# A gMLP's products over positions, from full-width operands to three products of split ones

## The chip, the core and the metric

The kernel runs on one core of a Trainium2 chip. The metric is the time of one execution on the device in microseconds (us); the median of several timed runs is compared. A profile is one further execution, recorded instruction by instruction. The engines are named as in the profile: PE (TensorE, matrix products), PEld (its weight loads, which run beside the products), DVE (VectorE), ACT (ScalarE), POOL (GpSimd) and SP (which here only issues DMAs). Each of them works through its own queue in order.

## What is computed

Two layers of a decoder trunk over 256 positions and 1024 features. The change lies in the third mixer of each layer, a gMLP:

```python
def chunked_spatial_gating(u_pre, v_pre, ln_g, ln_b, w_s, b_s):
    u = jax.nn.gelu(u_pre, approximate=False)
    v = layer_norm(jax.nn.gelu(v_pre, approximate=False), ln_g, ln_b)
    n = S // GMLP_CHUNK                      # 2 chunks of 128 positions
    vc = v.reshape(B, n, GMLP_CHUNK, GMLP_GROUPS, GMLP_GROUP_DIM)   # 8 groups of 128 features
    w_causal = w_s * tril[None]
    sp = jnp.einsum('gij,bnjgc->bnigc', w_causal, vc) + b_s.T[None, None, :, :, None]
    return u * sp.reshape(B, S, GMLP_WIDTH)
```

So each group has one 128x128 causal matrix over positions, which is applied to both chunks: 16 products of 128x128 by 128x128 per layer, 32 in all. Around them stand the large projections of the layer: the input projection to 12800 columns, the three branch projections, the output projection and a SwiGLU block, all in float32 accuracy.

## The kernel before

All large projections are done in a split form. An operand is parted into a high half of few mantissa bits (an ACT copy into the type fp32r) and the rest (a DVE subtraction); the function `split` (lines 196 and 197) emits these two instructions. A product then is three products of halves: high by high, high by low, low by high. `mm3` emits them (lines 268, 269, 270), for results that have features on the partitions; `toks` does the same for results with positions there (lines 288 to 290). `feat` makes one 256-feature block of a projection: 16 calls of `mm3` with 256 moving columns.

Weights stream in from DRAM as panels (1 MB each, tile `raw`), and each panel is cut into four pieces of 128x512, each split into `wh` and `wl`. The recording order is made by hand: a step of the list `steps` is one `feat` or a few `toks` with what follows on ACT and DVE, and while a step's products are emitted, `spend` counts their nanoseconds and calls `tick` once in 1300 of them. A tick emits one callback from the queue `hooks`, perhaps one part of the attention from `slow`, and zero to two pieces of weights, by how far the pieces are ahead of the products. Each engine then runs what it was given in this order, with semaphores between engines.

The stretch around the change, in each layer:

- `conv(j, which)` for j = 0 to 3 and which = 0, 1, 2: a `feat` each; with which = 2 the result on PSUM is multiplied into `cy` on DVE (line 744) and split into `yah` (ACT) and `yal` (DVE).
- `spatial`, called in `conv(2, 0)`, loads the causal matrices `ws` and the biases `bs` by hooks; two later hooks multiply the matrices by the triangle (line 485).
- `gu(j)` for j = 0 to 3, right after `conv(3, 2)`: first four products over positions for two groups and two chunks (line 764: stationary `gv`, which is v, moving `ws`, both plain float32), then the bias on DVE (line 768, tile `sp`), then a `feat` for u, its Gelu, the product u by `sp`, and the split into `ych` and `ycl`.

The attention of the same layer (`scores`, `turn`, `pv`) runs spread between these steps. Tiles of 128x512 come from two pools of slots, 48 and 24; `room` stops the making of pieces when few slots are left.

Of the kernel before, what the change touches and what calls it, by code (L numbers as in the profile page):

```python
# [12 lines left out]
F32R = mybir.dt.float32r  # L13
# [86 lines left out]
def trunk(ctx: ExitStack, tc: tile.TileContext, a, out):  # L100
    nc = tc.nc
# [16 lines left out]
    def flat(name, dt=F32, at=None):  # L118

        if at is None:  # L120
            y = sum(n.startswith("y") for n in home)
            at = int(not name.startswith(('va', 'qk', 'ws', 'bs')) and live[1] + (cnt["y"] - y if cnt["y"] else 0) < NS[1])
        live[at] += 1
        assert live[at] <= NS[at], (name, live)
        s = sl[at].tile([128, 512], dt, tag=f"slot{at}", name=name)
        home[s.tensor.name] = at
        return s

    def slot(name, dt=F32, at=None):
        return flat(name, dt, at).rearrange("p (b s) -> p b s", b=2)  # L130

    def free(*tiles):
        for s in tiles:
            live[home.pop(s.tensor.name)] -= 1
# [4 lines left out]
    def acc():  # L139
        return pa.tile([128, 512], F32, tag="acc", name="acc")  # L140
# [53 lines left out]
    def split(h, l, src):  # L194

        nc.scalar.activation(h, src, AF.Copy)  # L196
        V.tensor_tensor(l, src, h.bitcast(F32), op=OP.subtract)  # L197
# [20 lines left out]
    hooks = deque()  # L218
# [47 lines left out]
    def mm3(o, hl, rhs_h, rhs_l, first, last):  # L266

        nc.tensor.matmul(o, lhsT=hl[0], rhs=rhs_h, start=first, stop=False)  # L268
        nc.tensor.matmul(o, lhsT=hl[0], rhs=rhs_l, start=False, stop=False)  # L269
        nc.tensor.matmul(o, lhsT=hl[1], rhs=rhs_h, start=False, stop=last)  # L270

    def feat(p, rhs):

        ps = acc()
        for b in range(2):
            for k in range(p.kc):
                mm3(ps[:, b * S:(b + 1) * S], p.at(k, b * 128, 128), *rhs(k), k == 0, k == p.kc - 1)
                if b == 1 and k % 2 == 1:
                    used()
                if b == 0 or k < p.kc - 1:  # L280
                    spend(327)
        spend(327)
        return ps.rearrange("p (b s) -> p b s", b=2)
# [167 lines left out]
    def layer(L, steps):  # L451
        first, final = L == 0, L == DEPTH - 1
        w_in = a["w_in"][L]
        st = {}
# [40 lines left out]
        v_t = {}  # L495
# [50 lines left out]
        c = OFF_V  # L546
# [31 lines left out]
        for g in range(NG):  # L578
            c = OFF_ATT + (3 * g + 2) * GCOL
# [139 lines left out]
        def conv(j, which):  # L719
            def f(P):  # L720
                ps = feat(P[0], xf)
                cw = st["cw"]
                if which == 0:
                    if j == 0:
                        cnt["y"] = 20
                    if j == 2:
                        st["spatial"]()
                    st["c"] = slot("cc")
                    nc.scalar.activation(st["c"], ps, AF.Copy)
                elif which == 1:  # L730
                    z = st["c"]
                    y = st["y"] = slot("cy")
                    V.tensor_tensor(z, z, ps, op=OP.mult)
                    for i in (2, 1, 0):
                        for b in range(2):
                            w, n = cw[:, i, 2 * j + b:2 * j + b + 1], 2 - i
                            if n == 0:
                                V.tensor_scalar(y[:, b, :], z[:, b, :], w, None, op0=OP.mult)
                            else:
                                V.scalar_tensor_tensor(y[:, b, n:], z[:, b, :S - n], w, y[:, b, n:], op0=OP.mult, op1=OP.add)  # L740
                    free(z)
                else:
                    y = st["y"]
                    V.tensor_tensor(y, y, ps, op=OP.mult)
                    ya[j] = (slot(f"yah{j}", F32R, 1), slot(f"yal{j}", F32R, 1))
                    split(ya[j][0], ya[j][1], y)
                    free(y)
            return f
# [4 lines left out]


        yc = {}

        def gu(j):
            def f(P):
                sp = acc()
                for b in range(2):  # L760
                    g = 2 * j + b
                    for n in range(2):
                        vv = v_t[n, g // 4][:, (g % 4) * 128:(g % 4 + 1) * 128]
                        nc.tensor.matmul(sp[:, (2 * b + n) * 128:(2 * b + n + 1) * 128], lhsT=vv, rhs=st["wsT"][g // 4][:, g % 4, :], start=True, stop=True)  # L764
                s = slot("sp")
                for b in range(2):
                    g = 2 * j + b
                    V.tensor_tensor(s[:, b, :].rearrange("p (n i) -> p n i", n=2),
                                    sp[:, b * 256:(b + 1) * 256].rearrange("p (n i) -> p n i", n=2),
                                    st["bs"][g // 4][:, None, (g % 4) * 128:(g % 4 + 1) * 128].to_broadcast([128, 2, 128]), op=OP.add)  # L770
                ps = feat(P[0], xf)
                u = slot("u")
                nc.scalar.activation(u, ps, AF.Gelu)
                V.tensor_tensor(u, u, s, op=OP.mult)
                yc[j] = (slot(f"ych{j}", F32R, 1), slot(f"ycl{j}", F32R, 1))
                split(yc[j][0], yc[j][1], u)
                free(u, s)
                if j == 3:
                    free(*v_t.values(), *st["wsT"], *st["bs"])
            return f  # L780
# [41 lines left out]
        for j in range(4):  # L822
            n = slice(j * 256, (j + 1) * 256)
# [128 lines left out]
    for L in range(DEPTH):  # L952
        n = len(steps)
        starts[n] = layer(L, steps)
# [76 lines left out]
```

## Time and profile before

| | us |
|---|---|
| median of 3 timed runs (1135.79 to 1136.28) | 1135.81 |
| the profiled execution, its own time | 1134.36 |
| its span from first to last instruction | 1132.6 |
| PE busy | 1119.3 (99% of the span) |
| PEld busy | 1056.1 (93%) |
| DVE busy | 776.7 (69%) |
| ACT busy | 618.3 (55%) |
| mean granted clock of PE, as a share of full speed | 0.997 |

A row of the timeline gives the start in us from the start of the span, the duration, the engine, the line in the kernel, the operation, the tiles (out<-in), the shape and how many instructions the row joins. In a shape such as 128\*128 128x256 the first part is the stationary operand and the second the result. Consecutive products overlap in the engine's pipeline, so the pace of PE is read from start to start and not from the durations. In square brackets stands an idle time of the engine before the row and what ended it.

### The profile page before, as it was taken

What the parts mean: (1) busy time and instruction counts of PE and PEld (TensorE: products, weight loads), DVE (VectorE), ACT (ScalarE), POOL (GpSimd) and SP (SyncE); (2) the same over time, 40 slices, a digit from 0 to 9 for tenths busy, and PEclk for the clock granted to TensorE, in tenths of its full rate; (3) what the DMA queues carried; (4) which work ended last, traced back from release to release, by engine and by line L of the source; (5) the groups of instructions that cost most, each with busy time, mean ns of one, the idle gap of its engine ahead of it and who ended that gap; (6) DMA issues with size and microseconds to landing.
All of it is one profiled execution on the core that took longest, in us unless ns stands there. A gap on an engine that the chain in (4) does not pass through costs nothing.

```text
span 1132.6 us, 21868 instructions
## 1 busy us (share of the span) xinstructions
PE 1119.3 (99%) x8822; PEld 1056.1 (93%) x8822; DVE 776.7 (69%) x1401; ACT 618.3 (55%) x1139; POOL 58.2 (5%) x120
## 2 busy tenths in 40 slices
PE   9899999999999999999999999999999999999997
PEld 7799999999999899998888999999999998999985
DVE  6979786677555875556698677667675569655554
ACT  7565665666444374545387356566654445544550
POOL 0013200000002000000000232000000010000000
PEclk9999999999999999999999999999999999999999
DMA  9589555369557475546358575454666655745541
GB/s 323 167 269 295 161 170 192 124 212 309 170 178 272 160 262 187 181 156 242 125 179 297 170 224 167 150 197 150 210 237 206 199 192 190 257 157 179 186 149 38
DMA packets 175781, 223.35 MB, mean 197 GB/s; under 512 B 5824, under 2 KB 146368, under 8 KB 175680
## 3 DMA queue, kind: packets, MB, share of 16 engines
q1 hardware_dynamic: 169904, 209.36, 55.0%
q0 software_dynamic: 4672, 11.54, 3.5%
q8 instruction: 69, 1.13, 0.4%
q10 hardware_dynamic: 1104, 1.05, 0.3%
q14 instruction: 32, 0.26, 0.1%
HBM read 214.59 MB, written 1.05 MB: 190 GB/s over the span
## 4 chain that ended last, share of the span: by engine, by line
PE 98%; DVE 1%; DMA 0%; ACT 0%; issue 0%; ACTq 0%
PE acc L268 22%; PE acc L269 22%; PE acc L270 22%; PE acc L289 9%; PE acc L290 9%; PE acc L288 9%; PE trp L661 1%; PE acc L671 1%; PE trp L633 1%; PE acc L764 1%; PE trp L337 0%; PE trp L641 0%; PE acc L677 0%; DMA xT<-in_xT 0%; PE trp L872 0%
## 5 line engine op out<-in xcount | busy, mean ns | idle before, releaser
L197 DVE TENSOR_TENSOR wl<-raw,wh 128x512 fp32r<-128x512 f32 x776 | 496.7, 686 | 210.4 <-ACT wh L196 188.0
L268 PE MATMUL acc<-xh,wh 128*128 128x256 f32 x1856 | 517.0, 279 | 0.0
L270 PE MATMUL acc<-xh,wl 128*128 128x256 f32 x1856 | 512.5, 276 | 0.0
L269 PE MATMUL acc<-xl,wh 128*128 128x256 f32 x1856 | 512.5, 276 | 0.0
L196 ACT ACTIVATE wh<-raw 128x512 fp32r<-128x512 f32 x776 | 439.4, 623 | 103.3 <-PE acc L269 30.8
L268 PEld LDWEIGHTS acc<-xh,wh 128*128 128x128 f32 x1856 | 348.4, 188 | 1.2
L269 PEld LDWEIGHTS acc<-xl,wh 128*128 128x128 f32 x1856 | 348.5, 188 | 0.1
L270 PEld LDWEIGHTS acc<-xh,wl 128*128 128x128 f32 x1856 | 348.4, 188 | 0.0
L600 POOL DMA_DIRECT2D sw<-qk x96 | 47.3, 500 | 421.2 <-ACT qk L598 421.0
L288 PE MATMUL acc<-wh,hh 128*128 128x512 f32 x176 | 68.7, 390 | 0.0
L290 PE MATMUL acc<-wh,hl 128*128 128x512 f32 x176 | 68.5, 389 | 0.0
L289 PE MATMUL acc<-wl,hh 128*128 128x512 f32 x176 | 68.5, 389 | 0.0
L288 PE MATMUL acc<-wh,xh 128*128 128x512 f32 x128 | 50.9, 398 | 0.8 <-ACT wh L196 0.8
L289 PE MATMUL acc<-wl,xh 128*128 128x512 f32 x128 | 50.2, 392 | 0.2 <-DVE wl L197 0.2
L290 PE MATMUL acc<-wh,xl 128*128 128x512 f32 x128 | 50.3, 393 | 0.0
L289 PE MATMUL acc<-wl,xrh 128*128 128x512 f32 x96 | 38.3, 399 | 2.9 <-DVE wl L197 2.9
L290 PEld LDWEIGHTS acc<-wh,hl 128*128 128x128 f32 x176 | 33.0, 188 | 6.9
L288 PEld LDWEIGHTS acc<-wh,hh 128*128 128x128 f32 x176 | 33.0, 188 | 6.8
L289 PEld LDWEIGHTS acc<-wl,hh 128*128 128x128 f32 x176 | 33.1, 188 | 6.7
L290 PE MATMUL acc<-wh,xrl 128*128 128x512 f32 x96 | 38.3, 399 | 0.0
L288 PE MATMUL acc<-wh,xrh 128*128 128x512 f32 x96 | 38.1, 397 | 0.0
L797 ACT ACTIVATE sg<-acc 128x512 f32<-128x512 f32 x24 | 14.3, 597 | 42.7 <-PE acc L270 42.7
(157 smaller groups left out, 1331.9 us busy)
## 6 DMA issues: line engine op xcount, KB each, us to landing
raw<-in_w_in SPq DMA_DIRECT2D x98, 1024.0 KB, 5.0
raw<-in_w_gate SPq DMA_DIRECT2D x22, 1024.0 KB, 5.0
raw<-in_w_up SPq DMA_DIRECT2D x22, 1024.0 KB, 5.0
raw<-in_w_down SPq DMA_DIRECT2D x22, 1024.0 KB, 4.8
raw<-in_p_a SPq DMA_DIRECT2D x8, 1024.0 KB, 5.4
raw<-in_p_c SPq DMA_DIRECT2D x8, 1024.0 KB, 5.0
raw<-in_w_o SPq DMA_DIRECT2D x8, 1024.0 KB, 6.3
sw<-qk POOLq DMA_DIRECT2D x96, 64.0 KB, 3.3
```

The source lines that it names most:

```text
L196: nc.scalar.activation(h, src, AF.Copy)
L197: V.tensor_tensor(l, src, h.bitcast(F32), op=OP.subtract)
L268: nc.tensor.matmul(o, lhsT=hl[0], rhs=rhs_h, start=first, stop=False)
L269: nc.tensor.matmul(o, lhsT=hl[0], rhs=rhs_l, start=False, stop=False)
L270: nc.tensor.matmul(o, lhsT=hl[1], rhs=rhs_h, start=False, stop=last)
L288: nc.tensor.matmul(ps, lhsT=lhs[0], rhs=h, start=first, stop=False)
L289: nc.tensor.matmul(ps, lhsT=lhs[0], rhs=l, start=False, stop=False)
L290: nc.tensor.matmul(ps, lhsT=lhs[1], rhs=h, start=False, stop=last)
L600: nc.gpsimd.dma_start(sw[o:o + 32], r[i:i + 32])
L633: nc.tensor.matmul(ps[t, r][:, :S], lhsT=q[d, b, own[t]], rhs=k[d, b, :], start=(i == 0), stop=(i == 2))
L661: nc.tensor.transpose(ps[:, i * 128:(i + 1) * 128], p[:, i * 128:(i + 1) * 128], ident)
L797: nc.scalar.activation(s, ps, AF.Sigmoid)
```

## The change

`gu` no longer multiplies float32 tiles. A new function `vw_parts(j)` takes three slots, `vsh` and `vsl` for the halves of v (two chunks by 256 features) and `wsp` for both halves of two causal matrices, and puts two callbacks at the end of `hooks`: `values` splits v (two `split` of 128x256), `matrices` splits the two causal matrices (one `split` of 128x256). It is called for j = 0 at the end of the last `conv` step, and for j + 1 at the start of `gu(j)`. At its start, `gu(j)` takes callbacks from `hooks` until its own halves have been emitted. Each of the four products is an `mm3` with 128 moving columns.

```diff
@@ def conv(j, which): def f(P):
             ps = feat(P[0], xf)
             cw = st["cw"]
+            if which == 2 and j == 3:
+                vw_parts(0)
...
         yc = {}
+        vw = {}
+
+        def vw_parts(j):
+
+            vh, vl, w = (slot(n, F32R) for n in ("vsh", "vsl", "wsp"))
+            vw[j] = [vh, vl, w, False]
+            c = slice(j % 2 * 256, j % 2 * 256 + 256)
+
+            def values():
+                for n in range(2):
+                    split(vh[:, n], vl[:, n], v_t[n, j // 2][:, c])
+
+            def matrices():
+                split(w[:, 0], w[:, 1], st["wsT"][j // 2].rearrange("p g j -> p (g j)")[:, c])
+                vw[j][-1] = True
+
+            hooks.extend((values, matrices))
 
         def gu(j):
             def f(P):
+                while not vw[j][-1]:
+                    hooks.popleft()()
+                vh, vl, w, _ = vw.pop(j)
+                if j < 3:
+                    vw_parts(j + 1)
                 sp = acc()
                 for b in range(2):
-                    g = 2 * j + b
+                    c = slice(128 * b, 128 * b + 128)
                     for n in range(2):
-                        vv = v_t[n, g // 4][:, (g % 4) * 128:(g % 4 + 1) * 128]
-                        nc.tensor.matmul(sp[:, (2 * b + n) * 128:(2 * b + n + 1) * 128], lhsT=vv, rhs=st["wsT"][g // 4][:, g % 4, :], start=True, stop=True)
+                        mm3(sp[:, (2 * b + n) * 128:(2 * b + n + 1) * 128], (vh[:, n, c], vl[:, n, c]), w[:, 0, c], w[:, 1, c], True, True)
+                free(vh, vl, w)
                 s = slot("sp")
```

How this moves the instructions is shown at two engines, both at the border from `conv(3, 2)` to `gu(0)` in layer 0; layer 1 has the same rows with other numbers. In brackets stands which engine's semaphore an instruction waits for. First PE, of before:

```order
L270 MATMUL acc<-xh,wl 128x256
L764 MATMUL acc<-ws_2399,gv_274 128x128
L764 MATMUL acc<-ws_2399,gv_277 128x128
L764 MATMUL acc<-ws_2399,gv_274 128x128
L764 MATMUL acc<-ws_2399,gv_277 128x128
```

The same place on PE in the changed kernel:

```order
L268 MATMUL acc<-wsp,vsh 128x128 [waits Activation_49]
L269 MATMUL acc<-wsp,vsh 128x128 [waits DVE_49]
L270 MATMUL acc<-wsp,vsl 128x128
L268 MATMUL acc<-wsp,vsh 128x128
L269 MATMUL acc<-wsp,vsh 128x128
L270 MATMUL acc<-wsp,vsl 128x128
L268 MATMUL acc<-wsp,vsh 128x128
```

Twelve products stand where four stood, and the first two of them wait for ACT and for DVE, where the four waited for neither. Now DVE, from the multiplication of the last `conv` step's result on, before:

```order
L744 TENSOR_TENSOR cy<-cy,acc 128x512 [waits DVE_49,PE_49]
L197 TENSOR_TENSOR yal_2877<-cy,yah_2876 128x512 [waits Activation_49]
L768 TENSOR_TENSOR sp<-acc,bs_2401 128x256 [waits DMAHW6_49,PE_49]
L768 TENSOR_TENSOR sp<-acc,bs_2401 128x256
L652 RECIPROCAL ml<-ml 128x1 x2
```

The same place on DVE in the changed kernel (its line 746 is line 744 of before, 792 is 768):

```order
L746 TENSOR_TENSOR cy<-cy,acc 128x512 [waits DVE_49,PE_49]
L197 TENSOR_TENSOR yal_2880<-cy,yah_2879 128x512 [waits Activation_49]
L197 TENSOR_TENSOR vsl<-gv_274,vsh 128x256 [waits Activation_49]
L197 TENSOR_TENSOR vsl<-gv_277,vsh 128x256 [waits Activation_49]
L197 TENSOR_TENSOR wsp<-ws_2399,wsp 128x256 [waits Activation_49]
L792 TENSOR_TENSOR sp<-acc,bs_2401 128x256 [waits DMAHW6_49,PE_49]
L792 TENSOR_TENSOR sp<-acc,bs_2401 128x256
```

The three subtractions for `gu(0)` have come in behind the split of the last `conv` result and ahead of the bias; on ACT the three copies to `vsh`, `vsh` and `wsp` stand right behind the copy to `yah` in the same way.

## Rows read from the trace of the kernel before

**Rows 1.** The page: busy time of PE; shares of the chain that ended last

```profile
PE 1119.3 (99%) x8822; PEld 1056.1 (93%) x8822; DVE 776.7 (69%) x1401; ACT 618.3 (55%) x1139; POOL 58.2 (5%) x120
PE 98%; DVE 1%; DMA 0%; ACT 0%; issue 0%; ACTq 0%
```

**Rows 2.** Waits of PE over the whole span: us in total, times, longest

```profile
PE acc L289 <- DVE wl L197: 3.1, 2, 2.9
PE trp L990 <- DVE half_pi L985: 1.0, 1, 1.0
PE acc L288 <- ACT wh L196: 0.8, 1, 0.8
```

**Rows 3.** Timeline of PE at the first gu step, layer 0

```profile
211.24 0.28 PE L269 MATMUL acc<-xl,wh 128*128 128x256 f32 x1
211.35 0.28 PE L270 MATMUL acc<-xh,wl 128*128 128x256 f32 x1
211.47 1.05 PE L764 MATMUL acc<-ws,gv 128*128 128x128 f32 x8
212.28 0.37 PE L268 MATMUL acc<-xh,wh 128*128 128x256 f32 x1
212.48 0.28 PE L269 MATMUL acc<-xl,wh 128*128 128x256 f32 x1
```

**Rows 4.** Timeline of PE at a lone 32-column product (kick, L296)

```profile
242.19 0.28 PE L270 MATMUL acc<-xh,wl 128*128 128x256 f32 x1
242.30 0.30 PE L296 MATMUL trp<-con 128*128 128x32 f32 x2
...
242.64 0.28 PE L269 MATMUL acc<-xl,wh 128*128 128x256 f32 x1
```

**Rows 5.** Timelines of DVE and ACT around the first gu step, layer 0

```profile
209.91 3.09 DVE L197 TENSOR_TENSOR wl<-raw,wh 128x512 fp32r<-128x512 f32 x5
212.92 0.68 DVE L744 TENSOR_TENSOR cy<-cy,acc 128x512 f32<-128x512 f32 x1
214.30 0.69 DVE L197 TENSOR_TENSOR yal<-cy,yah 128x512 fp32r<-128x512 f32 x1 [0.70 <-ACT yah L196]
...
213.63 0.63 ACT L196 ACTIVATE yah<-cy 128x512 fp32r<-128x512 f32 x1 [2.78 <-DVE cy L744]
```

**Rows 6.** The same place in layer 1: timelines of PE, DVE and ACT

```profile
768.40 1.05 PE L764 MATMUL acc<-ws,gv 128*128 128x128 f32 x8
...
775.42 1.05 PE L764 MATMUL acc<-ws,gv 128*128 128x128 f32 x8
...
771.06 0.68 DVE L744 TENSOR_TENSOR cy<-cy,acc 128x512 f32<-128x512 f32 x1
772.44 0.69 DVE L197 TENSOR_TENSOR yal<-cy,yah 128x512 fp32r<-128x512 f32 x1 [0.70 <-ACT yah L196]
...
771.78 0.63 ACT L196 ACTIVATE yah<-cy 128x512 fp32r<-128x512 f32 x1 [3.08 <-DVE cy L744]
```

**Rows 7.** Groups by shape: splits of 128x256 from SBUF (busy us, mean ns | idle)

```profile
L976 ACT ACTIVATE xh<-xT 128x256 fp32r<-128x256 f32 x7 | 2.8, 402 | 0.0
...
L977 DVE TENSOR_TENSOR xl<-xT,xh 128x256 fp32r<-128x256 f32 x8 | 3.3, 419 | 0.0
```

**Rows 8.** PE's one long wait: timeline, and the window after it (granted clock third-last)

```profile
39.35 0.50 PE L289 MATMUL acc<-wl,xrh 128*128 128x512 f32 x1 [2.90 <-DVE wl L197]
...
41.31 0.63 PE L289 MATMUL acc<-wl,xrh 128*128 128x512 f32 x1
41.74 0.63 PE L290 MATMUL acc<-wh,xrl 128*128 128x512 f32 x1
...
40.30:43.72 3.42, 3.42 (x10) 2.64 (x9) 3.32 (x10) 0.00 (x0) 0.00 (x0) 0.50 0.22 57
```

**Rows 9.** Window around the first two gu steps: PE, PEld, DVE, ACT, POOL busy

```profile
208.00:222.00 14.00, 14.00 (x136) 13.87 (x136) 9.13 (x22) 7.73 (x15) 0.00 (x0) 1.00 0.45 147
```

## The prediction, made before the changed kernel ran

> **What bounds the kernel now.** I read the page first. PE is busy for 99% of the span, and the chain of waits that ended last runs over PE for 98% [rows 1]. The waits of PE say the same from the other side: three places, 4.9 us in all, none of them after the first steps of layer 0 [rows 2]. So PE is the bound everywhere near the change; a nanosecond added to PE's own queue, or a wait put into it, comes out at the end, and DVE and ACT time is free as long as nothing on PE waits for it. Next I read the timeline of PE at the place of the change, for its pace from start to start [rows 3], then those of DVE and ACT at the same moment, for how far they are behind PE [rows 5, 6]. The reader is to see there that DVE multiplies the last `conv` result at 212.92, some 1.5 us after PE has emitted it.
>
> **The products themselves.** The four products of a `gu` step have eight records: a float32 product is recorded twice. From L270 at 211.35 to L269 at 212.48 pass 1.13 us [rows 3]. Two ordinary steps of 0.113 are in that (211.24 to 211.35 is one), so the block takes 0.90, or 0.113 a record. After the change it is 12 records of one fp32r product each, with 128 moving columns and 128x128 weights. No row shows that form, so it is bounded:
> - Below, by columns alone: half of the 256-column step, 0.057.
> - Above, by what the same 128x128x128 product takes in float32 today, two records: 0.226.
> - Nearest row: the product at 242.30 has only 32 columns, but 128x128 weights. From L270 at 242.19 to L269 at 242.64 pass 0.45; less two ordinary steps, 0.22 is left for two records, 0.11 each [rows 4]. A quarter of the columns costs the same 0.113. What paces these is not the columns but the loading of 128 columns of weights, which the new form does once in each record too.
>
> I take 0.113. A block then takes 12 x 0.113 = 1.36 for 0.90: +0.45. Eight blocks: +3.6.
>
> Two rules of the Trainium skill are weighed here. "FP8 and Floating Point Precision", section TensorE Precision Notes, says that a true float32 product takes four passes through the array; three in place of four would save a quarter of a block, 0.23. The trace shows two records of 0.113 a product, which is four passes if columns paced them, but rows 4 say that they don't. "TensorE: Matmul & The Clock Gate", section Back-to-back issue gap, gives about 81 ns for each product of 128 columns with its load in a sustained stream; by that the sum below would be 3.0 lower. Both pull towards the lower bound, which is a rival below.
>
> **The wait that is added.** This is the larger term. `vw_parts(0)` is called after the `feat` of `conv(3, 2)`, and no tick follows before `gu(0)`, which therefore emits both callbacks itself, at once. In the changed order PE has nothing between the last product of `conv(3, 2)` and the first product over positions, and that one waits for ACT, the second for DVE. On DVE the three new subtractions stand behind L744, which needs PE's last product, and behind `yal`, which needs ACT's copy of L744's result. So PE waits for a chain that begins with its own last product. Placed on rows of before:
> - Layer 0 [rows 5]: DVE works off five `wl` until 212.92, then L744 until 213.60; ACT starts `yah` at 213.63, 0.03 later; DVE starts `yal` at 214.30. Five `wl` in 3.09, one alone 0.69: a step of 0.60, 0.09 less than the duration. The next subtraction starts at 214.90. One of 128x256 has 0.42 [rows 7], so a step of 0.33: 215.23, 215.56, and the last ends at 215.98. ACT's three copies of 0.40 [rows 7] follow `yah` from 214.26 and end by 215.46, ahead of the subtraction that needs the last. With 0.03 to 0.1 for the semaphore, PE goes on at about 216.04. It was there at 211.47 [rows 3]: a wait of 4.57.
> - Layer 1 [rows 6]: the same from `yal` at 772.44: 773.04, 773.37, 773.70, end 774.12, PE at 774.18. It was there at 768.40: 5.78. DVE is further behind PE here.
>
> The first product needs only ACT and runs inside the wait, so 11 follow: 11 x 0.113 = 1.24, less the 0.90 of before. The two `gu(0)` blocks cost 4.57 + 0.34 and 5.78 + 0.34, together 11.0. The other six blocks: 6 x 0.45 = 2.7. So far 13.7.
>
> **PE's clock after these waits.** The one long idle of PE in the trace, 2.90, is followed by a stretch of 3.42 with a granted clock of 0.50, 1.2 GHz; there 512-column products step by 0.43 (41.31 to 41.74) [rows 8], where twice the 0.113 is 0.23. Of 3.42 this loses 47%, 1.6. The two new waits are longer, so I expect a drop after each. But 1.24 of the restart is products paced by weight loads, which at half clock need 128 columns at 1.2 GHz, 0.107 each, no more than now, if the loads don't slow as well: (3.42 - 1.24) x 0.47 = 1.0. I take 1.2 a layer, 2.4 in all; the ends are 0 (the drop falls inside the wait) and 3.2.
>
> **What is free.** In the other steps the halves are emitted a step ahead. Three splits add 3 x 0.33 = 1.0 on DVE and 1.2 on ACT for each step of about 7.0 (768.40 to 775.42 [rows 6]). In 14.00 us of such steps DVE is busy for 9.13 and ACT for 7.73 [rows 9], so 2.0 and 2.4 go into idle time of 4.9 and 6.3; and each engine gains on PE by the 4 to 6 us that PE waits before. Three more slots, two sets at a time, let `room` hold a piece or two back, which leaves the weights nearer to their use; that lead was built while PE waited, and I cost it at nothing. If the cover is gone, the price is the 1.0 of DVE time in each of six blocks. No DMA is added or moved past another.
>
> **Sum.** 11.0 + 2.7 + 2.4 = +16.1. On the profiled execution's 1134.36 that is 1150.5; its span of 1132.6 would be about 1148.7. The median of the runs stands 1.45 above that execution, so the median becomes 1135.81 + 16.1 = 1151.9.
>
> **Rivals.**
> 1. *The columns pace it.* At 0.057 a product the `gu(0)` blocks cost 4.57 + 0.63 - 0.90 and 5.78 + 0.63 - 0.90, together 9.8, and the other six save 0.22 each, 1.3: 8.5, with the clock 10.9: 1146.7. For it speaks that this form is of another type than the records of rows 4; against it, that the weight loads of both types fill the same place. By the Trainium skill, the four passes of "FP8 and Floating Point Precision" come out at this same pace, and the 81 ns of "TensorE: Matmul & The Clock Gate" at 1148.9.
> 2. *The narrow form is slow.* If a 128-column fp32r product takes what the float32 one does now, 0.226, the blocks cost 6.2 and 7.4, and six times 1.8: 24.4, with the clock 26.8: 1162.6. Nothing in the trace speaks for it but that no fp32r product here has under 256 columns.
> 3. *DVE does not keep up.* The later blocks wait too, 1.0 each: +6.3, 1158.2. Against it rows 9.
> 4. *Not slower: the halves are ready when PE comes.* If the splits of `gu(0)` ran ahead of `yal`, inside the last `conv` step, the wait and the clock term would be gone, and by columns each block would save 0.22: 1135.81 - 1.8 = 1134.0. It takes both: with the wait gone and 0.113 the time is 1139.4, and with 0.057 it turns to slower as soon as the two waits pass 1.8 together. Against it stands the order of DVE and ACT in the changed kernel, where every one of the six instructions stands behind `yah` or `yal`.
>
> **How the numbers follow.** Forecast 0.70; rival 1 0.08, rival 2 0.09, rival 3 0.09, rival 4 0.04. The forecast's own range is 1148 to 1156: the clock from 0 to 3.2, the waits by 1 either way. The range for 8 in 10 reaches down to rival 1 and up to rival 3 and leaves out rivals 2 and 4: 1146 to 1159. A measurement of this kernel tells about 0.2% from no change, 2.3 us. Slower: all but rival 4, 0.96; of rival 4, at -1.8, most is "same", 0.03; faster 0.01.
>
> **What would show it.** In the changed kernel's profile: PE waits twice, at the first product over positions of each layer, released by DVE's `wsp` subtraction, 4.4 and 5.7 (the first product runs within); the start-to-start pace of the 128-column products is 0.113; the granted clock has two new stretches of 0.50 right after; no wait at the other six blocks. Wrong would be: waits under 3 us, which would mean that DVE and ACT reach the splits without `yal`; a pace far from 0.113; or PE waiting for `wl` after the `gu` steps, which would make the lead of the weights a cost that I left out.

## The result, and the profile after

The changed kernel takes 1154.26 us (median of 4 runs, 1153.43 to 1155.05) where the kernel before takes 1135.8 beside it: a ratio of 1.0166, with a 95% interval of 1.0153 to 1.0178, or +18.5. Run once more, in a later group of runs, it stood at 1.0171 (1.0157 to 1.0185). The forecast was 1151.9 with a range of 1146 to 1159.

The page of the changed kernel, in the lines that answer to [rows 1], and the waits of PE, which answer to [rows 2]:

```profile
span 1153.2 us, 21982 instructions
PE 1130.9 (98%) x8854; PEld 1066.6 (92%) x8854; DVE 785.7 (68%) x1425; ACT 626.3 (54%) x1163; POOL 58.1 (5%) x120
PE 90%; DVE 5%; ACT 3%; DMA 1%; issue 1%; ACTq 0%; SPq 0%
```

```profile
PE acc L268 <- ACT wsp L196: 8.4, 2, 4.8
PE acc L289 <- DVE wl L197: 3.1, 2, 2.9
...
PE acc L269 <- DVE wsp L197: 0.7, 2, 0.3
PE acc L288 <- ACT wh L196: 0.6, 1, 0.6
```

Two rows are new, both for `wsp`, twice each: the two layers. PE has 32 records more, 8854 for 8822, and no wait for a piece of weights that it did not have. The chain that ended last is now on DVE and ACT for 8% of the span, where it was 1%. Ahead of each of the two waits it stays on them for 34 us. These are its pieces at the two ends of that stretch in layer 0 (start, length, what):

```profile
182.34 0.02 DVE p L645
...
213.34 0.61 DVE cy L746
...
216.38 0.48 PE acc L269
```

So the lateness that PE meets at `gu(0)` is older than the last `conv` step: the chain goes back to the attention, at 182 (in layer 1 at 749).

The timeline of PE at the first `gu` step of layer 0, beside [rows 3]:

```profile
211.69 0.28 PE L270 MATMUL acc<-xh,wl 128*128 128x256 f32 x1
215.57 0.48 PE L268 MATMUL acc<-wsp,vsh 128*128 128x128 f32 x1 [3.60 <-ACT wsp L196]
216.38 0.48 PE L269 MATMUL acc<-wsp,vsh 128*128 128x128 f32 x1 [0.34 <-DVE wsp L197]
216.66 0.41 PE L270 MATMUL acc<-wsp,vsl 128*128 128x128 f32 x1
216.87 0.41 PE L268 MATMUL acc<-wsp,vsh 128*128 128x128 f32 x1
```

PE could have gone on at 211.81, one step of 0.113 after L270, and the second product starts at 216.38: a wait of 4.57, with the first product inside it. From there the products step by 0.21, not 0.113. In layer 1 the same rows:

```profile
777.40 0.28 PE L270 MATMUL acc<-xh,wl 128*128 128x256 f32 x1
782.51 0.48 PE L268 MATMUL acc<-wsp,vsh 128*128 128x128 f32 x1 [4.84 <-ACT wsp L196]
783.33 0.47 PE L269 MATMUL acc<-wsp,vsh 128*128 128x128 f32 x1 [0.34 <-DVE wsp L197]
```

From 777.51 to 783.33 are 5.82. DVE's timeline in layer 1 shows the chain, beside [rows 6]:

```profile
777.19 3.09 DVE L197 TENSOR_TENSOR wl<-raw,wh 128x512 fp32r<-128x512 f32 x5
780.20 0.68 DVE L746 TENSOR_TENSOR cy<-cy,acc 128x512 f32<-128x512 f32 x1
781.58 0.69 DVE L197 TENSOR_TENSOR yal<-cy,yah 128x512 fp32r<-128x512 f32 x1 [0.70 <-ACT yah L196]
782.18 0.75 DVE L197 TENSOR_TENSOR vsl<-gv,vsh 128x256 fp32r<-128x256 f32 x2
782.86 0.42 DVE L197 TENSOR_TENSOR wsp<-ws,wsp 128x256 fp32r<-128x256 f32 x1
```

The last subtraction ends at 783.28 and PE goes on 0.05 later. L746 does not wait for PE: it starts 2.7 after PE could have gone on (777.51), when the five `wl` before it are done. In layer 0 it starts 1.4 after (213.25, and PE could have gone on at 211.81). From its start to PE's going on pass 3.1 in both layers.

Two windows of the changed kernel, one from the middle of each wait on (the granted clock stands after the busy times of the five engines):

```profile
214.07:220.88 6.81, 4.97 (x22) 4.79 (x23) 3.25 (x10) 2.32 (x7) 0.00 (x0) 0.50 0.26 93
780.68:790.90 10.22, 8.05 (x36) 7.86 (x37) 4.48 (x13) 4.86 (x12) 0.00 (x0) 0.50 0.44 157
```

The clock is at its lower level, 1.2 GHz, for 6.8 and 10.2 us. It falls inside each wait and stays down after the wait's end, for 220.88 - 216.38 = 4.5 in layer 0 and 790.90 - 783.33 = 7.6 in layer 1. At the 47% of [rows 8] that is 2.1 and 3.6.

At the next step, `gu(1)` of layer 0, nothing waits, and the clock is at its upper level:

```profile
225.86 0.28 PE L270 MATMUL acc<-xh,wl 128*128 128x256 f32 x1
...
226.15 0.27 PE L270 MATMUL acc<-wsp,vsl 128*128 128x128 f32 x1
...
227.15 0.28 PE L270 MATMUL acc<-wsp,vsl 128*128 128x128 f32 x1
...
227.43 0.28 PE L269 MATMUL acc<-xl,wh 128*128 128x256 f32 x1
```

From 226.15 to 227.15 nine records pass in 1.00, 0.11 each. From L270 at 225.86 to L269 at 227.43 pass 1.57; less two ordinary steps, the block adds 1.34 where it added 0.90, which is 0.112 for each of its twelve records.

So the 20.6 between the two profiled spans are: 10.4 of waits (4.57 + 5.82), 5.7 of clock behind them, 2.6 for the longer blocks at the six later steps (6 x 0.44), 0.7 for the two first blocks at full clock (2 x 0.34), and 1.2 in tenths elsewhere, 0.3 of them before the change's place is reached. The two profiled executions stand at opposite ends of the runs of their kernels, hence 20.6 here and 18.5 between the medians.

### The profile page after: what moved, and what is told of

Read it like the earlier page. It is cut to its first block, busy times and chain, and to the rows that moved or that the text cites. A ratio compares the mean times of both kernels' runs of the same rounds, so it can differ in the third digit from the quotient of the medians.

```text
span 1153.2 us, 21982 instructions
## 1 busy us (share of the span) xinstructions
PE 1130.9 (98%) x8854; PEld 1066.6 (92%) x8854; DVE 785.7 (68%) x1425; ACT 626.3 (54%) x1163; POOL 58.1 (5%) x120
## 4 chain that ended last, share of the span: by engine, by line
PE 90%; DVE 5%; ACT 3%; DMA 1%; issue 1%; ACTq 0%; SPq 0%
PE acc L268 21%; PE acc L269 20%; PE acc L270 20%; PE acc L289 8%; PE acc L290 8%; PE acc L288 8%; DVE wl L197 2%; PE trp L661 1%; ACT wh L196 1%; ACT p L646 1%; PE acc L671 1%; DMA raw<-in_w_in 1%; DMA xT<-in_xT 1%; PE trp L633 0%; DVE cy L742 0%
## 5 line engine op out<-in xcount | busy, mean ns | idle before, releaser
L269 PE MATMUL acc<-xl,wh 128*128 128x256 f32 x1856 | 513.8, 277 | 0.0
L270 PE MATMUL acc<-xh,wl 128*128 128x256 f32 x1856 | 513.7, 277 | 0.0
L269 PEld LDWEIGHTS acc<-xl,wh 128*128 128x128 f32 x1856 | 349.7, 188 | 0.1
L270 PEld LDWEIGHTS acc<-xh,wl 128*128 128x128 f32 x1856 | 349.4, 188 | 0.0
L598 ACT ACTIVATE qk<-acc 128x512 f32<-128x512 f32 x24 | 14.3, 595 | 45.5 <-PE acc L270 43.2
```

The costliest lines, as they stand in the source:

```text
L598: nc.scalar.activation(r.rearrange("p b (m q) -> p b m q", m=4), by_residue(ps), AF.Copy)
```

## The experiments

The theory: PE waits because the splits stand behind `yal`; the wait lowers the clock; a product of 128 columns costs a weight load. The rivals: it is the added work on DVE and ACT, or the slots; or it is the products themselves. Ratios are to the kernel before on the same chip, whose median there was 1134.46, 1135.79 or 1135.07, one for each group of runs.

### The splits for gu(0) one step earlier

```diff
 def conv(j, which): def f(P):
+    if which == 1 and j == 3:
+        vw_parts(0)
     ps = feat(P[0], xf)
     cw = st["cw"]
-    if which == 2 and j == 3:
-        vw_parts(0)
```

> The changed kernel, but vw_parts(0) is called one step earlier, at the start of conv(3, 1); the halves for the later gu steps are emitted where the change puts them, one step ahead. Theory (the wait at gu(0) comes from the place of the splits behind yal): no wait at gu(0) in either layer. But then DVE and ACT do not catch up on PE there, and they run up to 8 us behind PE in the gu steps of before (DVE reads the sum of gu(1), layer 1, at 783.44, PE had made it by 776.5), so the later blocks should wait now: placed on rows of before, about 1.0 at gu(1) in layer 0 and 2 in layer 1, and some at gu(2) and gu(3); together 3 to 8 us, so 1142 to 1148. Rival (one step ahead is enough, only gu(0) was late): no wait at any block, the products alone, +3.6: 1139.4. Second rival (the time comes from the DVE and ACT work and the slots, not from a wait): about 1154, as the change.

Measured: 1146.77, a ratio of 1.0104 (1.0091 to 1.0118), +12.3 over the 1134.46 of its chip. The first blocks no longer wait. Others do; the timeline of PE at `gu(1)` in layer 1, and a window behind it:

```profile
782.20 0.28 PE L270 MATMUL acc<-xh,wl 128*128 128x256 f32 x1
784.25 0.33 PE L268 MATMUL acc<-wsp,vsh 128*128 128x128 f32 x1 [1.77 <-ACT wsp L196]
785.01 0.33 PE L269 MATMUL acc<-wsp,vsh 128*128 128x128 f32 x1 [0.43 <-DVE wsp L197]
```

```profile
785.75:789.10 3.35, 3.35 (x18) 3.35 (x17) 0.69 (x1) 3.32 (x5) 0.00 (x0) 0.50 0.93 310
```

The wait here is 2.7 (782.31 to 785.01), the one at `gu(1)` in layer 0 1.5, that at `gu(2)` in layer 0 0.8, together 5.0; the clock is down for 3.4 behind the longest of them. So the wait is from the place of the splits, as the theory has it, and a step ahead in the order is too little once DVE and ACT have not caught up at `gu(0)`: the rival with 1139.4 falls, and so does the one in which the work and not a wait costs the time.

### PE kept busy in the two long waits

```diff
     while not vw[j][-1]:
         hooks.popleft()()
+    if j == 0:
+        t = trp()
+        for _ in range((20, 26)[L]):
+            nc.tensor.matmul(t[:, :128], lhsT=ident, rhs=ident, start=True, stop=True)
```

> The changed kernel with PE kept busy during its two long waits: ahead of the first product of gu(0) stand 20 (layer 0) and 26 (layer 1) float32 products of 128x128 on the identity into a tile that nobody reads, two records of 0.113 each, 4.5 and 5.9 us, as long as the waits. Theory (after each wait the granted clock is 0.50 for a while, and that costs 5.5 us in the profiled run of the change): no stretch of 0.50 at gu(0), the twelve products step by 0.113 and not by 0.213, and the time is 5.5 below the change, 1148.8, with 1.5 either way. Rival (the clock's fall costs nothing beyond the wait): 1154.3 as the change.

Measured: 1148.95, a ratio of 1.0125 (1.0112 to 1.0139), where the change stands at 1.0166 and 1.0171. The timeline of PE in layer 0, and the window from the second product on:

```profile
211.69 4.62 PE L783 MATMUL trp<-con 128*128 128x128 f32 x40
216.07 0.31 PE L268 MATMUL acc<-wsp,vsh 128*128 128x128 f32 x1
216.28 0.33 PE L269 MATMUL acc<-wsp,vsh 128*128 128x128 f32 x1
216.44 0.27 PE L270 MATMUL acc<-wsp,vsl 128*128 128x128 f32 x1
216.55 0.28 PE L268 MATMUL acc<-wsp,vsh 128*128 128x128 f32 x1
```

```profile
216.10:222.00 5.90, 5.90 (x53) 5.86 (x53) 1.90 (x8) 2.65 (x6) 0.00 (x0) 1.00 0.02 5
```

Work that nobody needs, put where PE would have waited, makes the kernel faster by 0.41 to 0.46%, 4.7 to 5.2 us. The products start when they did, at 216.3, but the clock is at 1.00 and they step by 0.11. That is the price of the clock, by a second way: 5.7 was read from the first profile, and 4.7 is in the second, further down.

### The same with half of the filling

```diff
-        for _ in range((20, 26)[L]):
+        for _ in range((10, 14)[L]):
```

> As the run with PE kept busy in its long waits, but with half of the idle products: 10 and 14, 2.3 and 3.2 us of work ahead of the first product of gu(0), so that waits of about 2.3 and 2.7 are left. Theory A (the clock falls only after a long wait, such as the 2.90 of before or more): no new stretch of 0.50, the time of the full filling, 1149.0. Theory B (a wait of 2 or more is enough; in the run with the splits one step earlier PE waited 2.05 and 0.6 at gu(1), layer 1, and a stretch of 0.50 of 3.41 followed, while 0.7 and 0.6 at gu(1), layer 0, brought none): a stretch of 3.4 behind one or both, 0.5 to 1.6 each, 1149.5 to 1152.

Measured: 1153.26, a ratio of 1.0155 (1.0141 to 1.0169). The waits left are 2.4 (214.0 to 216.36) and 2.7 (781.7 to 784.42), and the clock fell behind both; two windows:

```profile
216.50:223.20 6.70, 6.70 (x32) 6.70 (x33) 1.80 (x7) 2.67 (x6) 0.00 (x0) 0.50 0.01 4
786.50:789.85 3.35, 3.35 (x19) 3.35 (x18) 1.10 (x6) 2.36 (x6) 0.00 (x0) 0.50 0.02 5
```

Theory A falls: both waits are under the 2.90 of before. Theory B is right that the clock falls behind such waits. Its price stands at the upper end of its range by the ratio (1.0155 of the 1134.46 that it was written with is 1152.0) and above it by the time; in the profile it was too low for layer 0, where the clock was down for 6.8 behind the shorter wait, and right for layer 1, with 3.4 behind the longer. Half of the filling gives almost nothing back.

### The wait without the new products

```diff
+    g = 2 * j + b
...
-    mm3(sp[:, ...], (vh[:, n, c], vl[:, n, c]), w[:, 0, c], w[:, 1, c], True, True)
+    vv = v_t[n, g // 4][:, (g % 4) * 128:(g % 4 + 1) * 128]
+    nc.tensor.matmul(sp[:, ...], lhsT=vv, rhs=w[:, 1, c].bitcast(F32), start=True, stop=True)
```

> The wait without the new products: all halves as in the change, but a gu step has the four float32 products of before, with v itself as the stationary and, as the moving operand, the low half of the causal matrices that DVE has just written, so that PE waits for DVE at the same place. (It leaves out the high half of the matrices.) Theory: the waits of the change at gu(0), 4.6 and 5.8, the fall of the clock behind them, and no more than the eight records a block of before: the change less 6 x 0.44 and 2 x 4 x 0.213, that is 4.4 less; the change stands at 1.0166 of before, so with before at 1134.5 as in the last call 1153.3 - 4.4 = 1148.9. Rival (the products are the greater part of the loss): under 1143.

Measured: 1150.16, a ratio of 1.0130 (1.0114 to 1.0145); 1148.9 on a base of 1134.5 is 1.0127. The row of PE's waits:

```profile
PE acc L789 <- DVE wsp L197: 10.1, 2, 5.7
```

The wait and the clock without the longer blocks make 13 of the 16.6 thousandths of the change; the rival, under 1143, falls.

### The new work without the wait: splits that nobody reads, and slots alone

The first has the four float32 products on `gv` and `ws`, with everything else of the change; the second takes the splits out as well and keeps the slots.

```diff
 # splits: the products of before
+    g = 2 * j + b
...
-    mm3(sp[:, ...], (vh[:, n, c], vl[:, n, c]), w[:, 0, c], w[:, 1, c], True, True)
+    vv = v_t[n, g // 4][:, (g % 4) * 128:(g % 4 + 1) * 128]
+    nc.tensor.matmul(sp[:, ...], lhsT=vv, rhs=st["wsT"][g // 4][:, g % 4, :], start=True, stop=True)
 # slots: besides
 def values():
-    for n in range(2):
-        split(vh[:, n], vl[:, n], v_t[n, j // 2][:, c])
+    pass
 def matrices():
-    split(w[:, 0], w[:, 1], ...)
     vw[j][-1] = True
```

> The changed kernel with the products of before: all halves are made, at the same places, but the four products of a gu step are the float32 ones on gv and ws, and nothing reads the halves. Theory (ACT and DVE work and slots are free): PE has the 32 products and no new wait, 1135.8, within 0.5. Rival (24 splits more on each engine, and pieces of weights held back by room for three more slots, make PE wait for wl): up to 1.0 in each of eight blocks, 1137 to 1144, with waits of PE for wl or wh in layer 0 after 212.

> The kernel with the float32 products and unread halves, without the splits: the three slots of each gu step are taken and given back as in the change, the callbacks do nothing. That kernel was 2.0 to 2.6 over before, where I had expected none; its PE waits 1.2 for DVE's reading of a sum at gu(2), layer 1. Theory (it is the added DVE work, 1.0 a step on an engine that is 8 us behind PE there): without it 1134.5 as before, and no wait of PE for sp. Rival (it is the slots: room holds pieces back, and the order of pieces moves): the same 2.0 as with the splits, 1136.5, with that wait still there.

Measured: with the splits 1137.08, 1.0020 (1.0011 to 1.0029); with the slots alone 1135.78, 0.9998 (0.9989 to 1.0007). The theory that the work is free missed by 0.2%, and the rival named the wrong wait. The timelines of PE and of DVE in layer 1 of the kernel with the splits:

```profile
786.00 1.05 PE L789 MATMUL acc<-ws,gv 128*128 128x128 f32 x8
788.25 0.36 PE L268 MATMUL acc<-xh,wh 128*128 128x256 f32 x1 [1.20 <-DVE sp L794]
...
787.36 0.75 DVE L794 TENSOR_TENSOR sp<-acc,bs 128x256 f32<-128x256 f32 x2
```

PE may begin the `feat` of `gu(2)` only in an accumulator that DVE has read, and DVE reads the sum of `gu(1)` from 787.36 to 788.11, while PE has been through with its block since about 786.9 (786.00 and eight records of 0.113). In the kernel before it read it just in time, and PE went on at 784.34:

```profile
783.48 1.05 PE L764 MATMUL acc<-ws,gv 128*128 128x128 f32 x8
784.34 0.36 PE L268 MATMUL acc<-xh,wh 128*128 128x256 f32 x1
...
783.44 0.75 DVE L768 TENSOR_TENSOR sp<-acc,bs 128x256 f32<-128x256 f32 x2
```

With the slots alone that wait is gone. The profiled spans with and without the splits, 1136.4 and 1134.3, are 2.1 apart; 1.5 of it come at this place and 0.6 at 229 to 233, in layer 0. So the work on DVE and ACT costs 2.1 to 2.6 (2.3 by the ratio, 2.6 by the medians) where PE does not wait elsewhere, and the slots cost nothing.

### Every set of halves two steps ahead, with split and with float32 products

```diff
 def conv(j, which): def f(P):
+    if which and j == 3:
+        vw_parts(which - 1)
     ps = feat(P[0], xf)
...
 def gu(j): def f(P):
-    if j < 3:
-        vw_parts(j + 1)
+    if j < 2:
+        vw_parts(j + 2)
```

> The changed kernel with every set of halves two steps ahead: vw_parts(0) at the start of conv(3, 1), vw_parts(1) at conv(3, 2), vw_parts(j + 2) in gu(j). Theory (the wait and the clock are all of the loss beyond the products, and a product costs a weight load, 0.112): no new wait of PE, granted clock 1.0 at all eight blocks, +0.44 a block, so +3.5: 1139.3, within 1. Rival (columns pace the products): 1134.0. Rival (DVE and ACT cannot carry it without the time that PE waited): PE waits for wl or wsp in the gu steps, 1141 to 1146.

> The halves two steps ahead, as in the run that had no wait for them, but with the four float32 products of before; nothing reads the halves. It parts that run's +6.3 (1.0055 of before): Theory (the products cost their loads, 0.44 a block and 3.5 in all, and the rest, 2.8, is DVE and ACT work that comes late for the weights): +2.8 over before, 1.0025, with PE's waits for wh and wl near 220 and none for wsp. Rival (the narrow products cost more than their own pace, by what they hold up around them): +1 or less, and the products 5 or more.

Measured: with the split products 1140.80, 1.0055 (1.0042 to 1.0067), +6.3; with the float32 products of before in the same order 1140.55, 1.0048 (1.0034 to 1.0062). PE's waits that are new, first of the kernel with the split products, then of the other:

```profile
PE acc L268 <- ACT wh L196: 0.8, 1, 0.8
PE acc L270 <- DVE wl L197: 0.2, 1, 0.2
```

```profile
PE acc L268 <- ACT wh L196: 1.3, 1, 1.3
PE acc L270 <- DVE wl L197: 0.5, 2, 0.2
```

No wait for `wsp` is left and no stretch of the lower clock at the `gu` steps. The split products add 0.44 a block, 3.5. Most of the rest are pieces of weights that come late. Compared product by product with the kernel before, the profile with float32 products is 4.5 longer: 2.3 of it arise at 220 to 223, where these waits stand, and 2.2 later, nearly all in layer 1, in steps of at most 0.5, which were not followed up. Compared with the slots alone, the profile with split products loses 1.4 at the same place, 0.8 less; its first two blocks had made PE 0.9 later there. So the longer blocks hide a part of the cost of the late pieces, the two kernels differ by less than their intervals, and the parts don't add up; neither expectation of the second run was right. Of the expectations of the first, the theory was too low by 1.5 (by the times) to 2.8 (by the ratio). The third, that DVE and ACT don't quite carry the work without the time that PE waited, comes nearest: the waits are for weights in the `gu` steps, and 1140.80 stands just under its 1141 to 1146. Even with no wait for its halves the change stays slower than the kernel before.

### Half of the moving columns

```diff
+    d = slice(128 * b, 128 * b + 64)
-    mm3(sp[:, (2 * b + n) * 128:(2 * b + n + 1) * 128], ..., w[:, 0, c], w[:, 1, c], True, True)
+    mm3(sp[:, (2 * b + n) * 128:(2 * b + n) * 128 + 64], ..., w[:, 0, d], w[:, 1, d], True, True)
...
```

> The kernel with every set of halves two steps ahead, with half of the moving columns: each of the twelve products of a block takes 64 columns of the causal matrices in place of 128 (the second 64 positions are left out, and the bias is added to the first 64 twice). Theory (a record costs the load of its 128x128 weights): the pace stays 0.112 from start to start, a block still adds 1.34. Rival (columns pace it, or the narrower form is slower by itself): 0.03 to 0.06 and a block of 0.4 to 0.7, or over 0.13.

The timeline of PE at `gu(1)`, layer 0:

```profile
221.21 0.28 PE L270 MATMUL acc<-wsp,vsl 128*128 128x64 f32 x1
...
222.21 0.28 PE L270 MATMUL acc<-wsp,vsl 128*128 128x64 f32 x1
```

From 221.21 to 222.21 nine records pass in 1.00, 0.111 each: the same with 64 columns as with 128. The one execution took 1142.81, where the same order with 128 columns took 1140.61 to 1142.26. The columns do not pace these products. A fixed cost of every record does not either, as a row of the kernel before shows, with 64 columns of weights and 64 moving columns:

```profile
222.35 0.40 PE L677 MATMUL acc<-pT,va 128*64 128x64 f32 x8
222.68 0.38 PE L268 MATMUL acc<-xh,wh 128*128 128x256 f32 x1
```

Eight records pass in 0.33, about 0.04 each. So the 0.112 goes with the 128x128 weights. That their load is what takes it fits all these rows, but no run varied the load alone.

### The change once more

> The change itself once more, on the chip of this call: 1.0166 of before, +18 to +19; the stretches of 0.50 behind the two waits as before, though their lengths may differ (6.83 and 10.24 in its first profile, 3.41 to 6.83 in others), and the time with them by 1.6 for each 3.41.

Measured: 1154.70, 1.0171 (1.0157 to 1.0185), +19.6, half a microsecond more than expected. The clock was down for 6.83 in both layers:

```profile
216.86:223.67 6.81, 5.83 (x26) 5.64 (x27) 2.96 (x10) 2.33 (x7) 0.00 (x0) 0.50 0.15 51
783.48:790.28 6.80, 5.14 (x23) 4.95 (x24) 3.25 (x10) 2.31 (x7) 0.00 (x0) 0.50 0.60 213
```

PE goes on at 218.32 and 785.62 here, so 5.4 and 4.7 of the stretches come after the waits: 2.5 and 2.2 at 47%, 4.7 in all where the first profile had 5.7. The clock's price is not the same in every execution. This profile has one more stretch that is longer, 6.83 where [rows 8] had 3.42, at the early wait, far from the change.

## Why the prediction was right, and which term was off

**The bound.** PE is the bound, and what is put into its queue comes out at the end: 10.4 of waits, 3.3 of products and 5.7 of clock are 19.4 of the 20.6 between the spans.

**The added wait.** Placed at 4.57 and 5.78, measured 4.57 and 5.82. The placing used rows of before alone: where DVE stands when PE is done, the step of a subtraction, and the order in the changed kernel. The order was the evidence that the wait must come; the run with the earlier splits shows that it is the place that makes it. One sentence of the working does not hold: that the chain begins with PE's own last product. DVE reached L746 1.4 and 2.7 after PE could have gone on, still busy with five pieces of weights, on a chain that goes back to the attention; only the other 3.1 of each wait is the chain from L746 on. The placing held because it started from where DVE stood.

**The products.** 0.113 expected, 0.112 measured; the block +0.45, measured +0.44. That rules out rival 1 (0.057) and rival 2 (0.226), and the run with 64 columns shows that the columns are not the reason. A float32 product costs 0.226 here and three split ones 0.336. The Trainium skill, page "FP8 and Floating Point Precision", section TensorE Precision Notes, counts four passes for a true float32 product; three passes in place of four would be less, and no run here shows that saving. The Trainium skill, page "TensorE: Matmul & The Clock Gate", section LDWEIGHTS (loading the stationary operand), gives the load's time in nanoseconds as its columns over 1.2, by estimate 107 for 128 columns: that is near the 0.112 at full clock. The 81 ns that the same page of the Trainium skill gives, in section Back-to-back issue gap, stand against 0.112 measured here.

**The clock, the term that was mis-sized.** 2.4 was expected, with 0 and 3.2 as its ends; 5.7 was measured, 4.7 in the second profile. Two steps of it failed. The length was taken from the one row of before, 3.42; behind the new waits the stretches were 6.8 and 10.2, 4.5 and 7.6 of them after PE had gone on. And I let the weight loads keep their pace at the lower clock, so that the twelve products would lose nothing; they step by 0.213 there and lose as much as all else. Filling the waits gave back 4.7 to 5.2. What decides the length of such a stretch was not settled: 3.4, 6.8 and 10.2 were all seen, a wait of 2.4 had a longer one than a wait of 2.7, and the wait of 5.8 had 10.2 in one execution of the change and 6.8 in another.

**What is free.** That the splits hide was right for the change, and for the reason given: PE's wait at `gu(0)` lets DVE and ACT catch up, and no later block waits. The price if that cover is gone was put at 1.0 in each of six blocks, which is 6.0 (the 6.3 of rival 3 is a slip). The runs have 5.0 of waits for `wsp` with the halves of `gu(0)` one step earlier, 2.1 to 2.6 for the splits in the place of the change, through an accumulator that DVE reads late, and 4.5 in the profile of the two-ahead order with float32 products, through late weights. In rival 4 I gave 1139.4 for a kernel without the wait; that price was left out there, and the measured +6.3 would be 1142.1.

**The sum.** 16.1 expected, 18.5 between the medians; the clock's 2.3 to 3.3 is about the difference. That the time lies within 1148 to 1156 all the same is in part luck: with the clock at its upper end, 3.2, the sum is 1152.7, and the 1154.26 is covered only by the room of 1 either way that was left for the waits, which needed none.

## What to carry to other kernels

Before a product is cut into more products of a cheaper type, look at whether columns or weight loads pace it: here, with 32, 64 and 128 columns per 128x128 load, every further record cost the same 0.11. Where operands are prepared a step ahead, see in the built order what stands in front of the preparation on its engine, and how far that engine is behind when the consumer arrives: a step ahead in the order is nothing if the first set is emitted by the consumer itself. And price a wait on the tensor engine with the clock behind it: here about half again as much as the wait.

## What the runs showed of the hardware that was not expected

- Records that the loads of 128x128 weights seem to pace slow down with the clock: 0.112 a record at the granted 1.00, 0.213 at 0.50.
- Behind PE's waits of 2.4, 2.7, 4.6 and 5.8 the clock was at 0.50 for 3.4, 6.8 or 10.2, and it fell before the end of the two longer ones; behind one of 1.5 (in the run with the earlier splits) it did not fall.
- Independent of the change, some executions have one more stretch of 0.50 near their start. The same window of the kernel with slots alone and of the kernel before:

```profile
7.70:11.08 3.38, 3.38 (x8) 2.62 (x9) 3.38 (x8) 3.09 (x8) 0.00 (x0) 0.50 1.06 388
```

```profile
7.70:11.08 3.38, 3.38 (x16) 2.79 (x15) 3.38 (x8) 3.01 (x8) 0.00 (x0) 1.00 1.07 395
```

Half as many products pass in it. The executions of these two kernels lie in two groups, near 1134.3 and 1135.9, and the profiled ones, 1136.07 with the stretch and 1134.36 without it, fit them; that it explains every such pair was not tried.
